# Starting every pair's weight sums early, and in another order, in a two-layer encoder trunk

## The chip, the core and the metric

The kernel runs on one core of one Trainium2 chip. The metric is the device time in microseconds (us) of one execution, the median of several. The engines named below are TensorE (PE, the matmuls), VectorE (DVE), ScalarE (ACT), GpSimd (POOL, here only an issuer of DMAs that add) and SyncE (SP, an issuer of plain loads). Each runs its own instructions strictly in the order of its queue.

## What is computed

528 tokens (16 learned ones and 512 of the input) of 1024 features pass through two layers, each of FFN, mixer, FFN; then a norm. Only the FFNs bear on the change:

```python
def rmsnorm(x, g):
    return x * lax.rsqrt(jnp.mean(x * x, axis=-1, keepdims=True) + EPS) * g

def swiglu(x, w_gate, w_up, w_down):
    return (jax.nn.silu(x @ w_gate) * (x @ w_up)) @ w_down

for l in range(DEPTH):                       # DEPTH = 2
    h = h + 0.5 * swiglu(rmsnorm(h, norm_gains[l, 0]), ffn_w_gate[l, 0], ffn_w_up[l, 0], ffn_w_down[l, 0])
    ...
    h = h + 0.5 * swiglu(rmsnorm(h, norm_gains[l, 2]), ffn_w_gate[l, 1], ffn_w_up[l, 1], ffn_w_down[l, 1])
```

The gate and up matrices are 1024 x 2816, the down matrix 2816 x 1024. The mixer (linear attention beside softmax attention) is the same code before and after.

## The kernel before

**Precision and products.** Operands are split into a high and a low part (`hi`, `lo`), and a product is three matmuls, hi*hi, hi*lo, lo*hi. The weight's high part is a cast on ACT (L343), its low part a subtraction on DVE (L344). The low and high parts live in four rotating buffers each, with one buffer apart for every fifth product, so that the parts of product n can be written when PE has finished product n−5 or so. An FFN is written (l, f): (0, 0), (0, 1), (1, 0), (1, 1).

**Pairs and units.** The 2816 hidden columns are 11 pairs of 256. For a pair, the products of gate and up with the two halves of the tokens are done as a 2 x 2 block product in Winograd's form, with seven products named "1" to "7" in place of eight. Their weights are blocks of the matrix or sums of blocks: "1" is w11, "2" is w12, "4" is w22, "5" is w21 + w22, "6" is s2 = w21 + w22 − w11, "7" is s3 = w21 − w11, and "3" is s4 = s2 − w12. Eight of the pairs also go, two at a time, through such a seven-product form of the down matrix; these are the four units of an FFN, numbered 11 to 14 in the same tables, and their weight sums are made in the same way. A unit is worked in while the pair behind its own two is computed: pairs 2, 4, 6, 8, and 3, 5, 7, 9 in (0, 0), which `lasts` names.

**How a sum is made.** The base, block 21, is loaded by SP into a tile of the pool `ws` (seven buffers), and POOL issues a DMA that adds block 22 onto it (`base`, `base_sum`): that is w21's sum. From w11, ACT writes −w11 into two more tiles (`negative`, L291). POOL's DMAs then add block 21 to one (s3) and w21's sum to the other (s2). In `first_sums` the two negatives come first, and s3's DMA before s2's. s4 starts from w12 likewise and adds s2. A DMA that needs another one's result is held on POOL until that one has landed, and what is behind it in POOL's queue is held too. The product that needs a sum has it cast on ACT like any weight, so the cast is held there until the sum has landed.

**When.** `Weights.use` runs once for each product, in the order of the table `ffn_steps`. It first takes from an agenda what has become due, then makes high and low parts some four products ahead, then fetches two further. The agenda holds (place, what, pair), what being 0 for the base's sum and 1 for `first_sums`. Units and some pairs (those after a last pair, and pair 2 of (0, 0)) are `early` (L251): their base is loaded LEAD = 2 loads sooner, and `first_sums` is issued as soon as w11 is fetched. For all others `first_sums` follows the making of w11's high and low parts (in `make`).

**Around a product.** Each group of matmuls at L749 goes into PSUM; `finished` then copies the partial result with a snapshot on ACT (L759) or adds it on DVE (L764) into one of two buffers of quarters, `c`. A later product that goes on accumulating in the same PSUM tile waits for that snapshot. When a pair's quarters are complete, `hidden` scales them by the norm's factor on DVE (L789), applies Silu on ACT (L512) and multiplies, and splits the result for the down product (L517 for the pairs outside the units). `high_priority` asks the scheduler to put instructions ahead of others in their engine's queue.

**The start.** In (0, 0) pairs 0 and 1 begin without the block form (`first_pair`), and the norm's sums (L541) are a few matmuls issued from inside it, with the factor from Ln, Exp and Square on ACT (L554, L512, L558) behind them. Copies of these pairs' results are at L715.

Of the kernel before, what the change touches and what calls it, by code (L numbers as in the profile page):

```python
# [43 lines left out]
NPAIR = FF // P // 2  # L44
# [21 lines left out]
LEAD = 2  # L66
# [6 lines left out]
def lasts(begin):  # L73
    return [2 * g + begin + 2 for g in range(SEVENS)]


def plains(begin):
    summed = [p for g in range(SEVENS) for p in unit(begin, g)]
    return [p for p in range(NPAIR) if p not in summed]
# [127 lines left out]
class Groups:  # L207


    def __init__(self, tc):  # L210
        self.tc, self.layer, self.groups, self.counts = tc, 0, {}, {}
# [16 lines left out]
class Weights:  # L228
# [3 lines left out]
    def __init__(self, nc, after, raw, hi, lo, wts, win, wdn):  # L232
        self.nc, self.raw, self.hi_pool, self.lo_pool, self.wts, self.win, self.wdn = nc, raw, hi, lo, wts, win, wdn
        self.sum_pool = None
        self.loads = []
        for t, col in zip(PLAN, COLUMN):
            if t[0] == "op":
                self.loads.append(t[1:])
            elif col % SLAB == 0:
                self.loads.append(col // SLAB)  # L240
        self.at = {load: i for i, load in enumerate(self.loads)}
        self.made, self.fetched, self.got, self.summed, self.raws, self.second = 0, 0, {}, {}, {}, {}
        self.pos, self.behind, self.after = 0, None, after
        ops = [i for i, load in enumerate(self.loads) if not isinstance(load, int)]
        self.apart = set(ops[4::5])
        self.extra = self.latest = None
        self.bases, self.agenda = [], []
        for i in ops:
            f, p, product = self.loads[i]
            if product == "1":  # L250
                early = p >= NPAIR or f == (0, 0) and p == 2 or p - 1 in lasts(f == (0, 0))  # L251
                at = i - LEAD * early
                self.bases.append((at, (f, p)))
                self.agenda += [(at, 0, (f, p))] + [(i, 1, (f, p))] * early
        self.bases.sort()
        self.agenda.sort()
# [45 lines left out]
        self.add(self.summed[f, i, "5"], self.dram(f, i, "22"))  # L302

    def first_sums(self, f, i, w):
        s3, s2 = [self.negative(f, i, n, w) for n in ("s3", "s2")]
        self.add(s3, self.dram(f, i, "21"))
        self.add(s2, self.summed[f, i, "5"])
        self.summed[f, i, "7"], self.summed[f, i, "6"], self.second[f, i] = s3, s2, s2

    def last_sum(self, f, i, w):  # L310
# [81 lines left out]
def build(tc, ctx, xt, wts, win, wdn, par, w2, const, umask, out):  # L392
# [13 lines left out]
    def after(ins):  # L406
        return tc.issue_after(ins) if ins is not None else nullcontext()
# [36 lines left out]
    def pair(second=False):  # L444
        return (slots["s2"] if second else pss).tile([P, 2, 512], F32, tag="s2" if second else "ss", name=nm("ss"))
# [65 lines left out]
    def act(*args, **kw):  # L511
        prev_act[0] = S.activation(*args, **kw).ins  # L512

    def split(src, tag_hi, tag_lo):
        n = src.shape[-1]
        hi, lo = slot(tag_hi, F32R, n), slot(tag_lo, F32R, n)
        S.copy(hi, src)  # L517
        V.tensor_tensor(lo, src, hi.bitcast(F32), ALU.subtract)  # L518
        return hi, lo
# [153 lines left out]
    def ffn(l, f, norm, done, following):  # L673

        x, rs, n = norm.x, None, live[0]
        w = n // 2
# [3 lines left out]
        last_pairs, plain_pairs = lasts(begin_block), plains(begin_block)  # L680
# [3 lines left out]
        def put_off(i, fn):  # L684
            later.setdefault(i, []).append(fn)
# [4 lines left out]
        def quarters():  # L690
            return slots["c"].tile([P, 4 * T], F32, tag="c", name=nm("c"))[:, : 4 * n].rearrange("p (j q c) -> p j q c", j=2, q=4)
# [3 lines left out]
        def first_pair(p, m):  # L695

            accs = [pair(m == "1") for _ in range(2)]
            blocks = [W.op((l, f), p, m + c) for c in "12"]
            for r, (hi, lo) in enumerate(blocks):
                for k, (first, second) in enumerate(zip(x, norm.second)):  # L700
                    for j, acc in enumerate(accs):
                        for i, (a, b) in enumerate(((hi, 0), (hi, 1), (lo, 0))):
                            for t, v in enumerate((first, second)):
                                last = TE.matmul(acc[:, t, :w], a[:, j, k], v[b][:, r], start=k == 0 and r == 0 and i == 0,
                                                 stop=k == len(x) - 1 and r == 1 and i == 2)
                    if (p, m, r, k) == (1, "2", 0, 1):
                        with after(last.ins):
                            factor.append(norm.rs("s2", urgent=False))
            st = made.setdefault(p, {})
            if "c" not in st:  # L710
                st["c"] = quarters()
            at = 2 * (m == "2")
            for j, acc in enumerate(accs):
                with tc.high_priority():
                    W.behind = S.copy(st["c"][:, j, at : at + 2], acc[:, :, :w]).ins  # L715
# [37 lines left out]
        def finished(p, product):  # L753
            st = made[p]
            acc = st[{"2": "Y", "5": "Z", "3": "Z"}.get(product, "X")][:, :, :w]

            def snapshot(q):
                with tc.high_priority():
                    snap = S.copy(st["c"][:, :, q], acc).ins  # L759
                if q == 3 and (p == 0 or p in last_pairs):  # L760
                    W.behind = snap

            def more(q, acc):
                V.tensor_tensor(st["c"][:, :, q], st["c"][:, :, q], acc, ALU.add)  # L764

            if product == "1":
                st["c"] = quarters()
                snapshot(0)
            elif product == "2":
                more(0, acc)  # L770
            elif product == "6":
                snapshot(1)
            elif product == "7":
                snapshot(3)
                more(3, st["Z"][:, :, :w])
            elif product == "4":
                hidden(st, p, 1)
            elif product == "3":
                with tc.high_priority() if p in last_pairs else nullcontext():
                    more(1, acc)  # L780
                hidden(st, p, 0)

        def hidden(st, p, m):

            c = st["c"]
            at = slice(2 * m, 2 * m + 2)

            def scale(to, src, cs):
                V.scalar_tensor_tensor(to, src, -0.5, rs[:, cs].unsqueeze(1).broadcast_to([P, 2, cs.stop - cs.start]),  # L789
                                       ALU.mult, ALU.mult)  # L790

            last = p in last_pairs
            at_end = steps.index(("P", p, "3")) if ("P", p, "3") in steps else now[0]
            if m and "X" in st:
                with tc.high_priority() if last else nullcontext():
                    scale(c[:, :, 2], st["X"][:, :, :w], slice(0, w))

            def gate():
                if m and "X" in st:
                    scale(c[:, :, 3], c[:, :, 3], slice(w, n))  # L800
                else:
                    both = c[:, :, at].rearrange("p j q c -> p j (q c)")
                    scale(both, both, slice(0, n))
                t, u = [c[:, j, at].rearrange("p q c -> p (q c)") for j in range(2)]
                act(t, t, AF.Silu)
                V.scalar_tensor_tensor(u, t, 0.5, u, ALU.mult, ALU.mult)
                if p in plain_pairs:
                    hid[2 * p + m] = split(u, *("tt" if p == 0 else "gg"))

            if last:  # L810
                put_off(at_end + (2 if m else 4), gate)
            else:
                gate()
            st["rows"] = st.get("rows", 0) + 1
            if st["rows"] == 2 and p not in plain_pairs:
                for i, piece in enumerate(forms(p, c)):
                    if last or i:
                        put_off((at_end + 6 if last else now[0]) + i, piece)
                    else:
                        piece()  # L820
# [738 lines left out]
```

## Time and profile before

| what | value |
|---|---|
| time, median of 3 runs | 2181.53 us (2181.1 to 2182.91) |
| the profiled execution's own time | 2182.33 us |
| its span in the trace | 2180.6 us |
| mean granted TensorE clock | 0.998 |
| PE busy | 99% of the span |
| DVE busy | 1712.3 us, 79% |
| ACT busy | 1369.9 us, 63% |
| POOL busy | 204.1 us, 9% |
| software DMAs (POOL's queue) | 121.65 MB, 31.3% of the 16 engines' span |
| hardware DMAs (SP's queue) | 195.13 MB, 26.3% |

The span is the time from the first to the last instruction in the trace; what lies outside it is the difference to the execution's time. Busy shares are means over all stages. A wait is idle time of an engine just before an instruction, put down to what ended it. `<-` in a row reads "is written from": `s<-w` on POOL is s2's add, `s<-win` is s3's, and `w<-win` is w21's.

### The profile page before, as it was taken

To read this page: it belongs to the slowest core of one execution; us is meant where nothing else is said; L and a number is where in the kernel's file an instruction comes from. 1 tells how busy PE (TensorE), PEld (TensorE's weight loads), DVE (VectorE), ACT (ScalarE), POOL (GpSimd) and SP (SyncE) were. 2 spreads that over 40 slices of the span, in tenths; PEclk is the share of its full clock that TensorE was granted. 3 is DMA by queue.
4 is the path that set the end of the run, shared out by engine and by line. 5 is a ranking of instruction groups with operands and counts; after the bars stand their busy time and mean duration, and the time that the engine had idled before them with its cause. 6 is when DMAs were issued, how large, how long until landed. Compare 5 with 4: busy or idle time off the path is not lost.

```text
span 2180.6 us, 40542 instructions
## 1 busy us (share of the span) xinstructions
PE 2148.4 (99%) x16572; PEld 2067.0 (95%) x16572; DVE 1712.3 (79%) x2627; ACT 1369.9 (63%) x2022; POOL 204.1 (9%) x236
## 2 busy tenths in 40 slices
PE   9999999999999999999999999999999999999998
PEld 9999999999999999999999999999888888999997
DVE  7888876677976678898689888775789867888885
ACT  8765655455784576666586666554557837666664
POOL 0111100000000011111011111000000001111110
PEclk9999999999999999999999999999999999999999
DMA  7788953211113678888578888632221137888871
GB/s 234 181 202 207 213 136 120 84 59 59 40 40 107 160 167 199 210 199 208 154 171 198 213 199 204 158 126 78 69 68 49 50 115 174 191 207 214 210 182 61
DMA packets 90748, 322.61 MB, mean 148 GB/s; under 512 B 10049, under 2 KB 12353, under 8 KB 90561
## 3 DMA queue, kind: packets, MB, share of 16 engines
q0 software_dynamic: 33408, 121.65, 31.3%
q1 hardware_dynamic: 55072, 195.13, 26.3%
q10 hardware_dynamic: 2080, 3.23, 0.4%
q8 instruction: 130, 2.13, 0.4%
q14 instruction: 58, 0.47, 0.1%
HBM read 257.06 MB, written 2.10 MB: 119 GB/s over the span
## 4 chain that ended last, share of the span: by engine, by line
PE 81%; DVE 6%; ACT 5%; DMA 4%; issue 3%; POOL 0%; SPq 0%; DVEq 0%; ACTq 0%; POOLq 0%
PE ss L749 32%; PE ss L868 14%; PE mm L529 14%; PE ss L529 11%; DMA s<-w 3%; PE sm L529 2%; DVE wlo L344 1%; DMA w<-win 1%; ACT whi L343 1%; PE sm L1238 1%; PE ss L1212 1%; ACT t L512 1%; PE sm L1256 1%; PE sm L1257 1%; PE ss L1213 1%
## 5 line engine op out<-in xcount | busy, mean ns | idle before, releaser
L749 PE MATMUL ss<-xc,whi 128*128 128x264 f32 (+1 forms) x4608 | 842.8, 284 | 11.1 <-ACT c L759 8.9
L749 PEld LDWEIGHTS ss<-xc,whi 128*128 128x128 f32 x4608 | 713.9, 189 | 14.6 <-ACT c L759 11.3
L749 PE MATMUL ss<-xc,wlo 128*128 128x264 f32 (+1 forms) x2304 | 653.8, 284 | 0.0
L749 PEld LDWEIGHTS ss<-xc,wlo 128*128 128x128 f32 x2304 | 434.4, 189 | 0.0
L529 PE MATMUL mm<-x,whi 128*128 128x264 f32 (+1 forms) x1712 | 383.3, 314 | 0.0
L343 ACT CAST whi<-w 128x1024 fp32r<-128x1024 f32 (+1 forms) x241 | 252.1, 1047 | 158.6 <-PE ss L749 64.9
L344 DVE TENSOR_TENSOR wlo<-w,whi 128x1024 fp32r<-128x1024 f32 (+1 forms) x241 | 292.6, 1215 | 56.6 <-ACT whi L343 55.9
L868 PE MATMUL ss<-g,whi 128*128 128x264 f32 (+1 forms) x1792 | 327.0, 283 | 0.0
L344 DVE TENSOR_TENSOR wlo<-s,whi 128x1024 fp32r<-128x1024 f32 x174 | 211.0, 1220 | 126.8 <-ACT whi L343 126.5
L343 ACT CAST whi<-s 128x1024 fp32r<-128x1024 f32 x174 | 180.9, 1047 | 182.5 <-DMA s<-w 102.8
L529 PEld LDWEIGHTS mm<-x,whi 128*128 128x128 f32 x1712 | 278.1, 188 | 15.7 <-DVE x L518 0.2
L868 PEld LDWEIGHTS ss<-g,whi 128*128 128x128 f32 x1792 | 277.0, 188 | 0.0
L529 PE MATMUL mm<-x,wlo 128*128 128x264 f32 (+1 forms) x856 | 264.4, 313 | 0.0
L868 PE MATMUL ss<-g,wlo 128*128 128x264 f32 (+1 forms) x896 | 253.9, 283 | 0.0
L343 ACT CAST whi<-raw 128x1024 fp32r<-128x1024 f32 x126 | 132.0, 1048 | 145.5 <-PE mm L529 69.5
L344 DVE TENSOR_TENSOR wlo<-raw,whi 128x1024 fp32r<-128x1024 f32 x126 | 153.8, 1221 | 78.7 <-ACT whi L343 78.0
L291 ACT ACTIVATE s<-w 128x1024 f32<-128x1024 f32 x174 | 179.9, 1055 | 9.7 <-DMA s<-s 9.7
L868 PEld LDWEIGHTS ss<-g,wlo 128*128 128x128 f32 x896 | 168.7, 188 | 0.0
L529 PEld LDWEIGHTS mm<-x,wlo 128*128 128x128 f32 x856 | 159.6, 188 | 7.4
L872 DVE TENSOR_TENSOR h<-h,ss 128x528 f32<-128x528 f32 (+1 forms) x224 | 153.2, 693 | 2.8
L529 PE MATMUL ss<-g,whi 128*128 128x264 f32 (+1 forms) x764 | 142.8, 302 | 1.3 <-ACT g L517 1.3
L529 PEld LDWEIGHTS ss<-g,whi 128*128 128x128 f32 x764 | 111.6, 188 | 6.9 <-ACT g L517 1.5
(300 smaller groups left out, 3340.6 us busy)
## 6 DMA issues: line engine op xcount, KB each, us to landing
w<-win SPq DMA_DIRECT2D x175, 512.0 KB, 5.7
raw<-wts SPq DMA_DIRECT2D x126, 512.0 KB, 3.4
w<-wdn SPq DMA_DIRECT2D x64, 512.0 KB, 6.8
s<-w POOLq DMA_DIRECT2D x58, 512.0 KB, 7.8
s<-s POOLq DMA_DIRECT2D x58, 512.0 KB, 5.7
w<-win POOLq DMA_DIRECT2D x42, 512.0 KB, 8.1
s<-win POOLq DMA_DIRECT2D x42, 512.0 KB, 7.5
w<-wdn POOLq DMA_DIRECT2D x16, 512.0 KB, 7.2
```

The lines of the kernel that those rows point to most:

```text
L291: self.nc.scalar.activation(t, w, AF.Copy, scale=-1.0)
L343: self.latest = nc.scalar.copy(hi[:, cs], w[:, cs]).ins
L344: nc.vector.tensor_tensor(lo[:, cs], w[:, cs], hi[:, cs].bitcast(F32), ALU.subtract)
L512: prev_act[0] = S.activation(*args, **kw).ins
L529: TE.matmul(acc.half[i][:width], lhs, rhs[:, acc.spans[i]], start=first, stop=last)
L749: TE.matmul(acc[:, j], a[:, j, k], b[:, at], start=bool(begin and k == 0 and i == 0), stop=k == len(x) - 1 and i == 2, skip_group_check=no ...
L868: TE.matmul(acc[:, j], a[:, 2 * half + j, k], b, start=bool(begin and k == 0 and i == 0), stop=k == 1 and i == 2, skip_group_check=not begin)
L872: V.tensor_tensor(to, to, acc, ALU.add)
L1212: TE.matmul(s[:n, i, :HF], lhs, kh[:, hs], start=True, stop=False)
L1213: TE.matmul(s[:n, i, :HF], lhs, kl[:, hs], start=False, stop=True)
L1238: TE.transpose(tp[:, j * w + u * n : j * w + (u + 1) * n], pr[:n, (2 * c2 + j) * P : (2 * c2 + j + 1) * P], ident[:n, :n])
L1256: TE.matmul(o[:, :w], vw, ph, start=i == 0, stop=False)
```

## The change

There are four edits. All pairs but pair 1 become early, so that `first_sums` of pairs 0, 2, 4, 6, 8, 10 (0, 3, 5, 7, 9 in (0, 0)) is issued when w11 is fetched, and the base of those pairs from 2 on is loaded two loads sooner; pair 1's base is loaded one load later. In `first_sums` s2's negative and add now come first, and then s3's. The norm's sums in (0, 0) are issued after the matmuls of k = 2 in place of k = 1, 12 matmuls later. And the last pair, 10, has its last add and its gated values at high priority.

```diff
--- before.py
+++ after.py
@@ -248,8 +248,8 @@
         for i in ops:
             f, p, product = self.loads[i]
             if product == "1":
-                early = p >= NPAIR or f == (0, 0) and p == 2 or p - 1 in lasts(f == (0, 0))
-                at = i - LEAD * early
+                early = p != 1
+                at = i + 1 if p == 1 else i - LEAD * (p > 1)
                 self.bases.append((at, (f, p)))
                 self.agenda += [(at, 0, (f, p))] + [(i, 1, (f, p))] * early
         self.bases.sort()
@@ -302,9 +302,10 @@
         self.add(self.summed[f, i, "5"], self.dram(f, i, "22"))
 
     def first_sums(self, f, i, w):
-        s3, s2 = [self.negative(f, i, n, w) for n in ("s3", "s2")]
+        s2 = self.negative(f, i, "s2", w)
+        self.add(s2, self.summed[f, i, "5"])
+        s3 = self.negative(f, i, "s3", w)
         self.add(s3, self.dram(f, i, "21"))
-        self.add(s2, self.summed[f, i, "5"])
         self.summed[f, i, "7"], self.summed[f, i, "6"], self.second[f, i] = s3, s2, s2
 
     def last_sum(self, f, i, w):
@@ -703,7 +704,7 @@
                             for t, v in enumerate((first, second)):
                                 last = TE.matmul(acc[:, t, :w], a[:, j, k], v[b][:, r], start=k == 0 and r == 0 and i == 0,
                                                  stop=k == len(x) - 1 and r == 1 and i == 2)
-                    if (p, m, r, k) == (1, "2", 0, 1):
+                    if (p, m, r, k) == (1, "2", 0, 2):
                         with after(last.ins):
                             factor.append(norm.rs("s2", urgent=False))
             st = made.setdefault(p, {})
@@ -776,9 +777,10 @@
             elif product == "4":
                 hidden(st, p, 1)
             elif product == "3":
-                with tc.high_priority() if p in last_pairs else nullcontext():
+                with tc.high_priority() if p in last_pairs + [NPAIR - 1] else nullcontext():
                     more(1, acc)
-                hidden(st, p, 0)
+                with tc.high_priority() if p == NPAIR - 1 else nullcontext():
+                    hidden(st, p, 0)
 
         def hidden(st, p, m):
```

Below, before and after are given apart, with the program's numbers in the names. A name such as s2_11_2 is s2 of FFN (1, 1), pair 2.

**ACT in (0, 0), from the cast of pair 2's s2 (product "6") on.** rs53 is the norm's factor, c63 pair 2's quarters, c34 pair 1's. Before:

```order
L343 CAST whi10_645<-s2_00_2_343 128x1024
L554 ACTIVATE rs53_682<-ss56_687,eps_86 128x528
L512 ACTIVATE rs53_682<-rs53_682 128x528
...
L291 ACTIVATE s3_00_3_792<-w11_00_3_651 128x1024
L291 ACTIVATE s2_00_3_794<-w11_00_3_651 128x1024
L759 COPY c63_824<-ss62_787 128x2x264
```

After:

```order
L344 CAST whi10_648<-s2_00_2_341 128x1024
L291 ACTIVATE s2_00_3_654<-w11_00_3_652 128x1024
L291 ACTIVATE s3_00_3_657<-w11_00_3_652 128x1024
L555 ACTIVATE rs53_700<-ss56_705,eps_86 128x528
...
L344 CAST whi12_794<-w11_00_3_652 128x1024
L513 ACTIVATE c34_579<-c34_579 128x528 x2
L518 CAST t60_789<-c21_319 128x528
L344 CAST whi13_839<-s3_00_2_344 128x1024
L344 CAST whi14_875<-w12_00_3_798 128x1024
L760 COPY c63_824<-ss62_793 128x2x264
```

The two negatives of pair 3 (L291) stood behind the norm's steps and the cast of w11; now they stand ahead of them, and the casts whi13 and whi14 and a pair of Silus (c34) stand ahead of the snapshot of c63.

**ACT in (1, 1), pair 2, from a snapshot of the pair before it on.** In (0, 1) and (1, 0) the same rows stand in the same order. Before:

```order
L759 COPY c1748_21433<-ss1734_21334 128x2x256
L343 CAST whi438_21527<-s2_11_1_21258 128x1024
L343 CAST whi440_21605<-w11_11_2_21533 128x1024
L759 COPY c1748_21433<-ss1734_21334 128x2x256
L554 ACTIVATE rs1753_21586<-ss1756_21591,eps_86 128x512
L343 CAST whi439_21601<-w21_11_1_21164 128x1024
L512 ACTIVATE rs1753_21586<-rs1753_21586 128x512
L291 ACTIVATE s3_11_2_21609<-w11_11_2_21533 128x1024
L558 ACTIVATE t1757_21597<-rs1753_21586 128x512
L291 ACTIVATE s2_11_2_21611<-w11_11_2_21533 128x1024
```

After:

```order
L760 COPY c1748_21433<-ss1734_21334 128x2x256
L344 CAST whi438_21530<-s2_11_1_21256 128x1024
L291 ACTIVATE s2_11_2_21560<-w11_11_2_21534 128x1024
L291 ACTIVATE s3_11_2_21563<-w11_11_2_21534 128x1024
L344 CAST whi440_21611<-w11_11_2_21534 128x1024
L760 COPY c1748_21433<-ss1734_21334 128x2x256
L555 ACTIVATE rs1753_21592<-ss1756_21597,eps_86 128x512
L344 CAST whi439_21607<-w21_11_1_21199 128x1024
L513 ACTIVATE rs1753_21592<-rs1753_21592 128x512
L559 ACTIVATE t1757_21603<-rs1753_21592 128x512
```

The two negatives of pair 2 stood among the norm's steps, behind the casts whi440 and whi439, s3's first; now both stand directly behind whi438, s2's first.

**POOL at the same place.** The DMAs that add, of pair 2 of (1, 1). Before:

```order
L296 DMA s4_11_1_21292<-s2_11_1_21258 128x1024
L296 DMA w21_11_2_21531<-win 128x1024
L296 DMA s3_11_2_21609<-win 128x1024
L296 DMA s2_11_2_21611<-w21_11_2_21531 128x1024
L296 DMA s4_11_2_21689<-s2_11_2_21611 128x1024
```

After:

```order
L296 DMA s4_11_1_21292<-s2_11_1_21256 128x1024
L296 DMA w21_11_2_21472<-win 128x1024
L296 DMA s2_11_2_21560<-w21_11_2_21472 128x1024
L296 DMA s3_11_2_21563<-win 128x1024
L296 DMA s4_11_2_21689<-s2_11_2_21560 128x1024
```

s2's add, which waits for w21's to land, now stands ahead of s3's, which does not.

PE has the same instructions as before, and its order changes in few places: in (0, 0) the norm's matmuls stand 12 later, and 17 matmuls of pair 3's product "1" (with whi12) stand ahead of pair 2's "6"; and in each other FFN four matmuls of one product change places with another's, early in pair 2's stretch. POOL has 240 DMAs as before.

## The prediction

> **What bounds the kernel now.** I began with the page's busy times, then asked the chain of waits for TensorE (PE) alone, because an engine that is busy nearly all the time can only give back what it waits.
>
> The page's first row:
>
> ```profile
> PE 2148.4 (99%) x16572; PEld 2067.0 (95%) x16572; DVE 1712.3 (79%) x2627; ACT 1369.9 (63%) x2022; POOL 204.1 (9%) x236
> ```
>
> PE is idle for 2180.6 − 2148.4 = 32.2 us of the span. Nothing but those 32.2 us, and stretches in which PE runs below its full clock, can be won without taking matmuls away, and the change takes none away. The waits of PE, longest first:
>
> ```profile
> PE ss L749 <- ACT c L759: 8.9, 7, 2.8
> PE ss L749 <- DVE c L764: 2.2, 4, 0.7
> PE ss L529 <- ACT g L517: 1.3, 1, 1.3
> PE ss L541 <- ACT c L715: 1.0, 1, 1.0
> ```
>
> Columns: total us, times, longest. These four are in the FFNs, where the change acts: matmuls at L749 wait until ScalarE (ACT) has copied the previous partial sum out of PSUM (the snapshot, L759) or VectorE (DVE) has added to it (L764). The same PE idle time by place, as busy time in the stretches that hold it:
>
> ```profile
> 40.00:50.00 10.00, 8.90 (x71) 8.48 (x71) 8.83 (x16) 9.90 (x17) 1.77 (x2) 1.00 0.98 255
> 70.00:80.00 10.00, 9.41 (x77) 9.20 (x76) 6.42 (x7) 5.67 (x7) 2.66 (x3) 1.00 0.97 229
> 180.00:190.00 10.00, 9.47 (x78) 9.26 (x77) 9.97 (x16) 8.93 (x12) 2.25 (x3) 1.00 1.02 208
> 800.00:812.00 12.00, 9.62 (x62) 9.00 (x61) 11.92 (x17) 8.80 (x12) 2.41 (x3) 0.86 0.95 170
> 1080.00:1090.00 10.00, 8.71 (x72) 8.49 (x71) 7.54 (x9) 7.77 (x10) 2.51 (x3) 1.00 0.68 181
> 1150.00:1160.00 10.00, 8.03 (x64) 7.60 (x63) 9.94 (x15) 7.37 (x11) 1.74 (x2) 1.00 0.97 164
> 1860.00:1880.00 20.00, 15.39 (x126) 14.79 (x125) 14.13 (x19) 12.23 (x17) 3.52 (x4) 1.00 0.85 188
> 2050.00:2060.00 10.00, 8.97 (x76) 8.77 (x76) 7.68 (x9) 8.17 (x10) 2.97 (x4) 1.00 0.83 148
> ```
>
> The first two columns are the stretch's length and PE's busy time; the difference is PE's idle time: 1.10, 0.59, 0.53, 2.38, 1.29, 1.97, 4.61 and 1.03 us, 13.5 in all. The three largest, at 800, 1150 and 1860, are one place of the program in three FFNs, pair 2. ACT's timeline at the largest (start, duration, line; in brackets the idle time before and what ended it):
>
> ```profile
> 1844.10 1.05 ACT L343 CAST whi<-s 128x1024 fp32r<-128x1024 f32 x1
> 1848.40 1.05 ACT L343 CAST whi<-w 128x1024 fp32r<-128x1024 f32 x1 [3.26 <-issue]
> ...
> 1866.77 1.05 ACT L343 CAST whi<-s 128x1024 fp32r<-128x1024 f32 x1 [5.55 <-DMA s<-w]
> ...
> 1871.18 0.58 ACT L759 COPY c<-ss 128x512 f32<-128x512 f32 x1
> ```
>
> The cast of s2 at 1866.77 waits 5.55 us for the sum's DMA, and the snapshot that PE needs stands behind it. The DMA was issued by GpSimd (POOL) only after ACT had made s3's negative and then s2's (start, duration; in brackets again what POOL waited for):
>
> ```profile
> 1842.26 0.89 POOL L296 DMA_DIRECT2D w<-win  x1 [6.24 <-DMA w<-win]
> 1853.34 0.88 POOL L296 DMA_DIRECT2D s<-win  x1 [10.19 <-ACT s L291]
> 1854.81 0.86 POOL L296 DMA_DIRECT2D s<-w  x1 [0.59 <-ACT s L291]
> ```
>
> It took 1866.77 − 1854.81 = 11.9 us. That is long: DMAs from and to the sums' tiles in the 40 us around, and then the load of the DMA engines (last two columns: share, GB/s):
>
> ```profile
> DMA to landing us min/median/max: 4.8/5.5/11.9
> ```
>
> ```profile
> 1848.00:1852.00 4.00, 3.99 (x32) 3.70 (x30) 2.33 (x3) 3.60 (x6) 0.00 (x0) 1.00 0.12 47
> 1852.00:1856.00 4.00, 4.00 (x36) 4.00 (x35) 3.09 (x5) 3.50 (x5) 1.74 (x2) 1.00 0.30 40
> 1856.00:1860.00 4.00, 4.00 (x36) 4.00 (x35) 4.00 (x6) 3.97 (x5) 0.00 (x0) 1.00 0.99 240
> ```
>
> The engines stood nearly empty until 1854, then s3's sum, s2's sum and the next unit's blocks all came at once. A sum issued some 6 us earlier has them to itself. That decides what this change is worth.
>
> **The change part by part.** *Early sums for pair 2, s2 first.* In the new order both negatives stand directly behind the cast at 1844.10, in the 3.26 us that ACT idles there; two of them (1.06 us each by a row below) fit in. POOL then waits only for the landing of the sum issued at 1842.26, 5.5 us in the median and 11.9 at worst, so s2's add goes out at 1848 to 1854. I take 1848, since the DMA share is 0.12 there. It then lands at 1853.5, and at 1860 even with 11.9 us; ACT asks for it at 1866.77 − 5.55 = 1861.2. So the 5.55 us are gone and the snapshot runs as soon as its product is done. Gains, each the whole idle time of its row: 2.38 + 1.97 + 4.61 = 8.96. The row at 2050 is the same thing for pair 8 (its snapshot followed a cast that came late): 1.03. At 70 it is pair 3 of the first FFN: 0.59. At 180 the pair was early already and only s2's place in the queue changes; between 0 and 0.53, I take 0.3.
>
> *What is late next there.* In each of the three places PE had a second wait, for a snapshot into a buffer that the previous pair frees when DVE has made its forms. These become due earlier too, as the gated values stood behind the same stall, but with little to spare. Unknown, between 0 and 1.46 us each; I take 0.4, nearer to zero since what they wait for also moves up: −1.2 in all.
>
> *The clock.* After the stall near 808 PE ran slowly for a while:
>
> ```profile
> 808.44 0.81 PE L749 MATMUL ss<-xc,whi 128*128 128x264 f32 x2 [1.46 <-ACT c L759]
> ...
> 809.26 0.64 PE L749 MATMUL ss<-xc,whi 128*128 128x264 f32 x2
> ...
> 811.89 0.40 PE L749 MATMUL ss<-xc,whi 128*128 128x264 f32 x2
> ...
> 812.25 0.41 PE L749 MATMUL ss<-xc,whi 128*128 128x264 f32 x2
> ```
>
> Three matmuls start every (811.89 − 809.26)/4 = 0.66 us, afterwards every 0.36. The five groups from 808.44 cost 3.45 instead of 1.8 us: 1.6 lost, and the row at 800 shows it as a granted clock of 0.86. No such loss follows the longer stall at 1860 (clock 1.00). I count the 1.6 as gained, since it stands right behind a wait that goes.
>
> The Trainium skill, "TensorE: Matmul & The Clock Gate", section "What's actually happening", states that the clock halves after a whole idle window of about 3.4 us. The trace does not agree: here PE lost the clock after a gap of 1.46 us, and kept it (1.00) in the row that holds its longest, 2.8 us. By the rule alone the slow stretch would not be due to the stall, would stay, and the sum would be 1.6 us less.
>
> *Steady pairs (4, 6, 8 and the like).* Their sums also move up by some 7 us; PE has no wait in those stretches, so nothing is gained. What could be lost is a rival below.
>
> *End of the second FFN.* ACT's timeline, with PE waiting for the gated value at 1085.43:
>
> ```profile
> 1081.56 1.05 ACT L343 CAST whi<-w 128x1024 fp32r<-128x1024 f32 x1 [1.01 <-DMA w<-win]
> ...
> 1084.46 1.06 ACT L291 ACTIVATE s<-w 128x1024 f32<-128x1024 f32 x1
> 1085.43 0.61 ACT L517 CAST g<-c 128x528 fp32r<-128x528 f32 x1
> ```
>
> With the priority, s3's negative goes behind it; s2's takes the place of the cast at 1081.56 and waits for the same block. The value comes 0.97 us sooner: 1.0 of 1.29 us.
>
> *First FFN, norm sums one part on.* PE's wait of 1.0 us at L541 ends when the copy of ACT's first row below has run, at 45.17 + 0.59 = 45.76; the sums now come 12 matmuls later (1.5 us at 0.36 for three), when the copy is done, and the 1.0 is gained. But the early sums of pair 3 now stand ahead of the norm's own activations:
>
> ```profile
> 45.17 0.59 ACT L715 COPY c<-ss 128x528 f32<-128x528 f32 x1
> ...
> 48.17 0.70 ACT L554 ACTIVATE rs<-ss,eps 128x528 f32<-128x528 f32 x1
> ...
> 53.04 0.65 ACT L512 ACTIVATE c<-c 128x528 f32<-128x528 f32 x1 [0.57 <-DVE c L789]
> ...
> 56.99 1.06 ACT L343 CAST whi<-w 128x1024 fp32r<-128x1024 f32 x1
> ...
> 58.96 2.02 ACT L291 ACTIVATE s<-w 128x1024 f32<-128x1024 f32 x2
> 60.88 0.60 ACT L759 COPY c<-ss 128x528 f32<-128x528 f32 x1
> ```
>
> The two at 58.96 occupy ACT until 60.88 (1.9 us). They move to 48.2, so the norm's first step begins at about 50.1; a cast now stands between the norm's steps (1.0), and the scaled values and what follows come some 2.9 us later: the Silu at 53.04 near 55.9, the cast at 56.99 near 59.9, its DVE half near 62. The snapshot of 60.88 also has two more casts (1.9) and two Silus (1.1) ahead of it, and the negatives no longer: 60.88 + 2.9 − 1.9 + 1.9 + 1.1 = 64.9, done at 65.5. PE's next product into that buffer now starts as the snapshot ends, 61.5. Less the 1.0 us that goes it would be there at 60.5; 17 matmuls (2.1 us) of another product, the cast's, now stand ahead of it, so 62.6. PE waits 65.5 − 62.6 = 2.9 us, for the cast's halves first and the snapshot then: net −1.9. From both sides: nothing if DVE and ACT catch up, 4 us if the cast's lateness, some 1.5 for PE, comes on top instead of running beside the snapshot's.
>
> The sum: 8.96 + 1.03 + 0.59 + 0.3 + 1.0 + 1.6 − 1.2 − 1.9 = 10.4 us. From the profiled execution's 2182.33 us (span 2180.6 and 1.7 outside it) that is 2171.9; the median of the runs, 2181.53, lies 0.8 lower, so I predict 2171.1.
>
> **The rivals.** *A new stall early on, and clock lost elsewhere.* The first FFN pays 4 us (net −3), the second waits stay whole (3 x 1.46 = 4.4), and the 1.6 of clock is lost at a new place: 11.9 − 3 − 4.4 = 4.5 gained, 2181.5 − 4.5 = 2177.0. For it: ACT is busy for 9.90 of 10 us at 40. Against: in the next stretch shown, at 70, it is busy for 5.67.
>
> *The sum is still late.* If POOL is held at the head of its queue until the pair's first sum lands, and that landing takes 11.9 us too, s2's add leaves at 1854.2, when it left before, and lands at 1866: PE's waits of pair 2 and the slow clock stay, and of the rest come 1.03 + 0.59 + 1.0 − 1.9 = 0.7 us: 2180.8. Against: the empty DMA engines at 1848. The Trainium skill, "DMA: Bandwidth & Descriptors", section "Issuing engines are not separate DMA queues", says that all queues interleave on the same 16 engines; the row at 1856 (0.99) agrees.
>
> *Slower: negatives ahead of what they wait for.* 23 more pairs (five in the first FFN, six in each other) have negatives on ACT that wait for a freshly loaded block, with casts and snapshots behind them. The page's row of these loads, then the load of a steady pair's block (SyncE) and the ACT row behind which its negatives now stand:
>
> ```profile
> w<-win SPq DMA_DIRECT2D x175, 512.0 KB, 5.7
> ```
>
> ```profile
> 832.52 0.33 SPq L285 DMA_DIRECT2D w<-win  x1
> ```
>
> ```profile
> 842.17 1.05 ACT L343 CAST whi<-s 128x1024 fp32r<-128x1024 f32 x1 [1.20 <-DMA s<-w]
> ```
>
> The load lands after 5.7 us in the median; the negatives come 843.2 − 832.5 = 10.7 us after its issue. Up to there nothing happens. If loads grew to 11.9 us, the longest seen here, each of the 23 would hold ACT for 1.2 us, and as PE is 99% busy up to 28 us would come back: 2171.1 + 28 = 2199. It outweighs the gain of 10.4 us from 10.7 + 10.4/23 = 11.2 us on. Against: 5 us of reserve.
>
> *The change does nothing*, the stalls only passing to the next wait: it is the second rival's time, and counted there.
>
> **How the numbers follow.** Forecast 0.62, early stall and lost clock 0.17, sum still late 0.14, slower 0.07. About 0.2% (4.4 us) is what a measurement of this kernel can tell from no change. The first two are faster by more than that, except for the weakest part of the early stall: faster 0.78, same 0.15, slower 0.07. The lower end takes all 13.5 us, the clock's 1.6, and a new stall of nothing: 15.1, 2166.4, rounded to 2166.0. The upper end takes in the early stall's 2177.0 with 1.5 us more for a longer one, 2178.5; beyond it lie most of the two last rivals.
>
> **What would show it.** Right: no ACT wait on "DMA s<-w" before the cast of s2 in pair 2 of the last three FFNs; PE's waits on L759 down from 8.9 to about 3, most of it near 61 to 65; a granted clock of 1.00 at 808; POOL's s2 sum issued near 1848 in its stretch; PE's wait at L541 gone. Wrong: ACT waiting on "DMA w<-win" in steady pairs, PE's total busy time grown by slow clock, or the waits near 800, 1150 and 1860 still there under another name.

## The result and the profile after

The changed kernel takes 2168.1 us (median of 6 runs, 2166.94 to 2168.73) against 2181.32 for the kernel before (6 runs): a ratio of 0.9938, 95% interval 0.9925 to 0.9951. That is 13.2 us less; 10.4 were forecast. Between the two profiled executions it is 2182.33 − 2168.02 = 14.3 us.

The page's first row of the changed kernel, and PE's waits in the FFNs. Line numbers are one or two higher than before (L749 is now L750, L759 is L760):

```profile
PE 2145.2 (99%) x16572; PEld 2066.7 (95%) x16572; DVE 1714.5 (79%) x2627; ACT 1370.5 (63%) x2022; POOL 204.7 (9%) x236
```

```profile
PE ss L750 <- DVE c L765: 1.5, 3, 0.9
...
PE ss L750 <- DVE wlo L345: 0.8, 1, 0.8
...
PE ss L530 <- ACT g L518: 0.4, 1, 0.4
```

The span is 2166.2 us, so PE idles 21.0 us in place of 32.2. The 8.9 us of waits for a snapshot are gone altogether, the 2.2 for DVE's add and the 1.0 at L541 too, and 1.3 became 0.4. New are 0.8 us for a weight's low part, near 60 us, and 1.5 us for DVE's add in three places, all in the last FFN.

ACT in pair 2 of the last FFN, the place whose rows of before stand in the prediction:

```profile
1834.21 1.05 ACT L344 CAST whi<-s 128x1024 fp32r<-128x1024 f32 x1
1835.16 2.00 ACT L291 ACTIVATE s<-w 128x1024 f32<-128x1024 f32 x2
...
1838.47 1.05 ACT L344 CAST whi<-w 128x1024 fp32r<-128x1024 f32 x1 [1.30 <-PE ss L750]
...
1852.22 2.19 ACT L344 CAST whi<-s 128x1024 fp32r<-128x1024 f32 x2
...
1857.14 0.58 ACT L760 COPY c<-ss 128x512 f32<-128x512 f32 x1
```

The negatives fill the gap of 3.26 us, as the order had them, and the cast at 1852.22 no longer waits. POOL there, and how long the two adds took to land (the last column):

```profile
1838.45 0.87 POOL L296 DMA_DIRECT2D s<-w  x1 [5.27 <-DVE t L537]
1839.01 1.21 POOL L296 DMA_DIRECT2D s<-win  x1
```

```profile
s<-w POOLq DMA_DIRECT2D x1, 512.0 KB, 4.8
s<-win POOLq DMA_DIRECT2D x1, 512.0 KB, 9.3
```

s2's add lands 4.8 us after its issue in place of 11.9, 9 us before ACT wants it. Up to here the forecast reads well. The experiments show that moving the sums up was one of two ways to this, and not needed.

### The profile page after: what moved, and what is told of

Same layout as the page of the kernel before. It is cut to its first block, busy times and chain, and to the rows that moved or that the text cites. A ratio compares the mean times of both kernels' runs of the same rounds, so it can differ in the third digit from the quotient of the medians.

```text
span 2166.2 us, 40569 instructions
## 1 busy us (share of the span) xinstructions
PE 2145.2 (99%) x16572; PEld 2066.7 (95%) x16572; DVE 1714.5 (79%) x2627; ACT 1370.5 (63%) x2022; POOL 204.7 (9%) x236
## 4 chain that ended last, share of the span: by engine, by line
PE 83%; DVE 7%; ACT 4%; DMA 3%; issue 2%; SPq 0%; POOL 0%; DVEq 0%; POOLq 0%; ACTq 0%
PE ss L750 35%; PE mm L530 14%; PE ss L870 13%; PE ss L530 11%; PE sm L530 3%; DMA w<-win 1%; DMA s<-w 1%; DVE wlo L345 1%; PE sm L1240 1%; DMA w<-wdn 1%; PE ss L732 1%; ACT t L513 1%; PE ss L1214 1%; PE sm L1258 1%; ACT whi L344 1%
## 5 line engine op out<-in xcount | busy, mean ns | idle before, releaser
L750 PE MATMUL ss<-xc,whi 128*128 128x264 f32 (+1 forms) x4608 | 839.9, 284 | 1.5 <-DVE c L765 1.5
L750 PEld LDWEIGHTS ss<-xc,whi 128*128 128x128 f32 x4608 | 712.6, 188 | 3.2 <-DVE c L765 2.2
L750 PE MATMUL ss<-xc,wlo 128*128 128x264 f32 (+1 forms) x2304 | 653.2, 284 | 0.8 <-DVE wlo L345 0.8
L750 PEld LDWEIGHTS ss<-xc,wlo 128*128 128x128 f32 x2304 | 433.6, 188 | 1.0 <-DVE wlo L345 1.0
L870 PEld LDWEIGHTS ss<-g,whi 128*128 128x128 f32 x1792 | 277.1, 188 | 0.0
L291 ACT ACTIVATE s<-w 128x1024 f32<-128x1024 f32 x174 | 178.1, 1053 | 1.2 <-DMA w<-win 1.1
L296 POOL DMA_DIRECT2D w<-win x42 | 44.2, 1053 | 812.9 <-DVE g L519 383.1
```

The costliest lines, as they stand in the source:

```text
L291: self.nc.scalar.activation(t, w, AF.Copy, scale=-1.0)
L296: self.nc.gpsimd.dma_start(t, src, accum_op=ALU.add)
L750: TE.matmul(acc[:, j], a[:, j, k], b[:, at], start=bool(begin and k == 0 and i == 0), stop=k == len(x) - 1 and i == 2, skip_group_check=no ...
L870: TE.matmul(acc[:, j], a[:, 2 * half + j, k], b, start=bool(begin and k == 0 and i == 0), stop=k == 1 and i == 2, skip_group_check=not begin)
```

## The experiments

### Each edit alone

The first edit alone, on the kernel before:

```diff
-                early = p >= NPAIR or f == (0, 0) and p == 2 or p - 1 in lasts(f == (0, 0))
-                at = i - LEAD * early
+                early = p != 1
+                at = i + 1 if p == 1 else i - LEAD * (p > 1)
```

> The kernel before with the first edit alone: all pairs but pair 1 early, s3 still ahead of s2 in the queue, norm sums and priorities as before. Early theory (the sum leaves sooner because its negative stands in ACT's gap): PE's waits on the snapshot at about 800, 1150 and 1860 us are gone (9 us), the slow clock at 808 too (1.6), the stretch near 60 us gets a wait of 1 to 3 us and the 1.0 at 45 stays; the time is 9 to 12 us below the kernel before. Queue theory (s2's place ahead of s3 does it): half of those waits or more stay, 5 us or less below.

Measured: 2171.23 us, ratio 0.9957 (0.9944 to 0.9969), 9.9 us less than the 2181.16 beside it. The waits of pair 2 are gone; the first FFN has three waits, at 46, 62 and 64 us (1.4, 0.6, 1.4 us).

The second edit alone:

```diff
-        s3, s2 = [self.negative(f, i, n, w) for n in ("s3", "s2")]
+        s2 = self.negative(f, i, "s2", w)
+        self.add(s2, self.summed[f, i, "5"])
+        s3 = self.negative(f, i, "s3", w)
         self.add(s3, self.dram(f, i, "21"))
-        self.add(s2, self.summed[f, i, "5"])
```

> The kernel before with the second edit alone: s2's negative and add ahead of s3's, nothing earlier otherwise. Early theory: s2's add leaves 1.5 us sooner and still meets the same crowd of transfers, so ACT's wait for it in pair 2 of the last FFN falls from 5.55 to some 3 to 4 us and PE keeps most of its waits there; 2 to 5 us below the kernel before. Queue theory: the waits at 800, 1150 and 1860 go, 9 us or more below.

Measured: 2166.62 us, ratio 0.9939 (0.9926 to 0.9951), 14.5 us less. So this edit alone does what the whole change does, and the expectation of 2 to 5 us was wrong. The waits of pair 2 are gone although no sum is started at an earlier product. The two gains are the same gain: either edit removes the wait, and together they can't remove it twice.

The other two edits alone:

```diff
-                    if (p, m, r, k) == (1, "2", 0, 1):
+                    if (p, m, r, k) == (1, "2", 0, 2):
```

> The kernel before with the third edit alone, the norm sums 12 matmuls later. Both theories: the 1.0 us wait at 45 us goes, or half of it comes back a little later; all else stays: 0 to 1 us below the kernel before, which the measurement can't tell. Its waits of pair 2 stay, and show whether the slow clock follows them again: if it follows any stall, it shows at one or more of 808, 1157, 1872 us; if it is tied to the first, at 808 alone.

```diff
-                with tc.high_priority() if p in last_pairs else nullcontext():
+                with tc.high_priority() if p in last_pairs + [NPAIR - 1] else nullcontext():
                     more(1, acc)
-                hidden(st, p, 0)
+                with tc.high_priority() if p == NPAIR - 1 else nullcontext():
+                    hidden(st, p, 0)
```

> The kernel before with the fourth edit alone, the last pair's gated values at high priority. The wait of 1.3 us for the gated value at 1086 falls to 0.3 to 0.5; all else stays, 1 us below the kernel before, within what can be measured. Its waits of pair 2 stay, and are a second look at the slow clock.

Measured: norm sums later 2181.25 us, ratio 1.0008 (0.9999 to 1.0017); priority 2181.21 us, ratio 1.0002 (0.9993 to 1.0011). Neither moves the time by itself. With the norm sums later, the wait at 45 us goes, and 2.6 + 0.6 us of waits come a little later in the first FFN. The priority leaves the wait for the gated value at 1.2 us; it was expected to fall to 0.3 to 0.5.

### Undoing parts of the change

Pair 2 of the last three FFNs late again:

```diff
-                early = p != 1
-                at = i + 1 if p == 1 else i - LEAD * (p > 1)
+                early = p != 1 and not (p == 2 and f != (0, 0))
+                at = i + 1 if p == 1 else i - LEAD * (p > 1 and early)
```

> The changed kernel with pair 2 of the last three FFNs not early (its base two loads later as before, its sums behind the making of w11), all else changed. Early theory: ACT waits for s2's DMA in these three places again and PE for the snapshot, 5 to 9 us and perhaps the slow clock come back: 2173 to 2179. Queue theory: s2 is still first in the queue, so the time stays within 2 us of 2168.

Measured: 2169.82 us (0.9952, 0.9939 to 0.9964), 1.7 us above the changed kernel, though the intervals of the two ratios overlap; of its waits on the snapshot 0.2 us is back. So at the very place on which the forecast rested, moving the sums up isn't needed once s2 goes first.

No first edit at all, the other three kept:

```diff
-                early = p != 1
-                at = i + 1 if p == 1 else i - LEAD * (p > 1)
+                early = p >= NPAIR or f == (0, 0) and p == 2 or p - 1 in lasts(f == (0, 0))
+                at = i - LEAD * early
```

> The changed kernel without its first edit: only the units and the pairs that were early before are early; s2 first, norm sums later and the priority stay. If the queue place does the work and the early sums add nothing that PE waits for, the three waits of pair 2 stay gone, the waits at 1908 and 1968 and the one near 60 us are gone too, and the time is 2164 to 2167. If the early sums bring a part of their own, it is 2169 or more.

Measured: 2166.6 us (0.9936, 0.9923 to 0.9948; 2165.28 to 2166.97 in 5 runs), 1.5 us below the changed kernel, with no wait at all between 30 and 100 us and none on DVE's add. The kernel before took 2180.54 us beside it, 0.8 less than beside the changed kernel, so the two ratios can't be told apart. In the traces the span is 2165.1 us against 2166.2, with one stretch of slow clock near 550 us in each: there the early sums cost a little more than they bring.

### What s2 first changes on the chip

In the kernel before, s3's and s2's adds and two plain loads (SyncE, the next unit's blocks) are issued within 1.5 us. Their landing times, first of the kernel before, then of s2 first alone:

```profile
w<-wdn SPq DMA_DIRECT2D x2, 512.0 KB, 8.3
s<-win POOLq DMA_DIRECT2D x1, 512.0 KB, 5.4
s<-w POOLq DMA_DIRECT2D x1, 512.0 KB, 11.9
```

```profile
w<-wdn SPq DMA_DIRECT2D x2, 512.0 KB, 8.5
s<-w POOLq DMA_DIRECT2D x1, 512.0 KB, 5.5
s<-win POOLq DMA_DIRECT2D x1, 512.0 KB, 10.6
```

The two adds change places; the loads land about as before (8.5 us in place of 8.3). Over the whole program the page's medians say the same, before and with s2 first alone:

```profile
s<-w POOLq DMA_DIRECT2D x58, 512.0 KB, 7.8
...
s<-win POOLq DMA_DIRECT2D x42, 512.0 KB, 7.5
```

```profile
s<-w POOLq DMA_DIRECT2D x58, 512.0 KB, 5.5
...
s<-win POOLq DMA_DIRECT2D x42, 512.0 KB, 10.3
```

s3 pays, and has the time: PE has no wait for it in this kernel. I took this for the place in POOL's queue alone, and tested that by exchanging the two adds on POOL and leaving ACT's order as it was:

```diff
         s3, s2 = [self.negative(f, i, n, w) for n in ("s3", "s2")]
-        self.add(s3, self.dram(f, i, "21"))
-        self.add(s2, self.summed[f, i, "5"])
+        first = self.nc.gpsimd.dma_start(s2, self.summed[f, i, "5"], accum_op=ALU.add).ins
+        with self.after(first):
+            self.add(s3, self.dram(f, i, "21"))
```

> The kernel before with the two adds of first_sums exchanged on GpSimd alone; on ScalarE s3's negative still comes first, so s2's add can leave no sooner than before. Whole-transfer theory (a sum second in GpSimd's queue lands only after the first one's transfer, 5.4 against 11.9 us in the kernel before): s2's add lands 5 to 6 us after its issue, the waits on the snapshot at 800, 1150 and 1860 go, and the time is 11 to 14 us below the kernel before, like that of s2 first. Rival (what counts is that the negative and so the issue come 1.5 us sooner): s2 still lands late and the gain is 4 us or less.

Measured: 2175.56 us, ratio 0.998 (0.9971 to 0.9989), 5.0 us less: the whole-transfer theory falls as it was put. In pair 2 of the last FFN:

```profile
w<-wdn SPq DMA_DIRECT2D x2, 512.0 KB, 5.1
s<-w POOLq DMA_DIRECT2D x1, 512.0 KB, 9.3
```

```profile
1859.02 1.05 ACT L344 CAST whi<-s 128x1024 fp32r<-128x1024 f32 x1 [2.93 <-DMA s<-w]
```

First in its queue s2 still needs 9.3 us, and now the loads are quick. Halving what stands ahead of it in the kernel before:

```diff
-        self.add(s3, self.dram(f, i, "21"))
+        self.add(s3[:64], self.dram(f, i, "21")[:64])
```

> The kernel before, with s3's add moving 64 of the 128 partitions: it leaves out half of that sum, so that what stands ahead of s2's add in the queue is half as large, and the order of everything stays. Theory (s2's transfer waits for the bytes ahead of it): s2's add lands about 2.5 us sooner than in the kernel before where the two leave together (11.9 to about 9.5 us in pair 2 of the last FFN, ACT's wait there 5.55 to about 3), and a third to two thirds of the 13 us come back: 2172 to 2177. Rival (what counts is the order or the number of transfers, not their size): s2 still lands at 11 us or later there, and the time stays at 2180 or above.

Measured: 2176.22 us, ratio 0.9975 (0.9964 to 0.9985), 5.1 us less. s2 lands after 10.2 us and ACT waits 3.85 in place of 5.55: the bytes ahead count, but by less than expected. The next run leaves s3's add out:

```diff
-        self.add(s3, self.dram(f, i, "21"))
```

> The kernel before without s3's add: it leaves that sum out, so s2's add has nothing ahead of it or beside it in GpSimd's queue, and leaves at the same place of ACT's order as before, 0.4 us behind two plain loads of the next unit (SyncE's queue). If s3 alone makes s2 late, s2 lands after 5.5 us in pair 2 of the last FFN and all waits there go, 12 to 14 us below the kernel before. If the two loads ahead of it cost it as well, as in the kernel with the queue exchanged (9.3 us, loads 5.1), s2 still lands after 8 us or more there, some of PE's waits stay, and the time is 5 to 9 us below the kernel before.

Measured: 2172.15 us, ratio 0.9961 (0.9947 to 0.9975), 8.3 us less. POOL, SyncE and ACT in pair 2 of the last FFN:

```profile
1847.94 0.87 POOL L296 DMA_DIRECT2D s<-w  x1 [13.19 <-ACT s L291]
```

```profile
1847.56 0.80 SPq L285 DMA_DIRECT2D w<-wdn  x2
```

```profile
1857.32 1.05 ACT L342 CAST whi<-s 128x1024 fp32r<-128x1024 f32 x1 [2.96 <-DMA s<-w]
```

With nothing else in POOL's queue s2 still takes 9.3 us, since two loads left 0.4 us ahead of it. So, at this place: 5.5 us when s2 leads, 9.3 with the loads ahead, 11.9 with the loads and s3 ahead. The first edit alone fits in: there s3's add leaves at 1839.13, s2's at 1841.80, the loads at 1843.32, and s2 lands after 5.9 us. And why the loads leave just then shows in ACT, SyncE and POOL of s2 first alone:

```profile
1843.55 1.05 ACT L291 ACTIVATE s<-w 128x1024 f32<-128x1024 f32 x1
...
1845.02 1.06 ACT L291 ACTIVATE s<-w 128x1024 f32<-128x1024 f32 x1
```

```profile
1846.10 1.26 SPq L285 DMA_DIRECT2D w<-wdn  x2
```

```profile
1845.01 0.87 POOL L296 DMA_DIRECT2D s<-w  x1 [10.85 <-ACT s L291]
1846.47 0.87 POOL L296 DMA_DIRECT2D s<-win  x1 [0.60 <-ACT s L291]
```

The second negative ends at 1846.08 and the loads are issued at 1846.10: it is the last reader of w11, and frees the buffer that they wait for. SyncE's waits name it, in the kernel before as well:

```profile
SPq L285 <- ACT s L291: 3.7, 1, 3.7
```

In the kernel before the last negative is s2's, so the same event lets go the loads and, 0.4 us later, s2's add (SyncE in the kernel before; s2's add was at 1854.81):

```profile
1854.43 0.85 SPq L285 DMA_DIRECT2D w<-wdn  x2
```

With s2's negative first, its add leaves 1.1 us ahead of the loads. That is the edit's worth here. The Trainium skill, "DMA: Bandwidth & Descriptors", section "Queues, rings and completion order", states that each engine goes round between the queues packet by packet. By an even share, an estimate from that rule, an add 0.4 us behind two loads would not end long after them; in the run without s3 it landed 9.3 us after its issue, the loads 4.3 and 6.0 after theirs. At this place whoever comes first was served first, beyond an even share; why is not shown.

### What the early sums cost and bring

Pairs 4, 6 and 8 of the last FFN late again:

```diff
-                early = p != 1
-                at = i + 1 if p == 1 else i - LEAD * (p > 1)
+                early = p != 1 and not (f == (1, 1) and p in (4, 6, 8))
+                at = i + 1 if p == 1 else i - LEAD * (p > 1 and early)
```

> The changed kernel with pairs 4, 6 and 8 of the last FFN not early. The changed kernel's trace shows PE waiting 0.92 and 0.36 us for a DVE add (L765) in the last FFN at 1908 and 1968, and it loses 2.2 us there against the kernel before. Theory: the two negatives, now ahead of the cast of the previous unit's form on ACT (1.9 us), make DVE's forms and the add behind them late; then these waits go, the wait of 1.0 us on the snapshot at about 2040 returns for pair 8, and the time is 2166 to 2167. Rival: the waits come from pair 2's faster stretch ahead of them, and stay; the time is 2168 to 2169.5.

Measured: 2166.81 us (0.9937, 0.9923 to 0.995), and PE has no FFN wait left between 1800 and 2100 us; the 1.5 us are gone, and the wait for pair 8's snapshot didn't return. The time lies 1.3 us below the changed kernel, but the runs of the two overlap. The chain in the changed kernel, pair 4, ACT, then DVE, then PE:

```profile
1897.02 2.00 ACT L291 ACTIVATE s<-w 128x1024 f32<-128x1024 f32 x2
1898.93 0.60 ACT L831 CAST g<-c 128x512 fp32r<-128x512 f32 x1
```

```profile
1907.60 0.69 DVE L765 TENSOR_TENSOR c<-c,ss 128x512 f32<-128x512 f32 x1
```

```profile
1907.15 0.28 PE L750 MATMUL ss<-xc,wlo 128*128 128x256 f32 x1
1908.34 0.51 PE L750 MATMUL ss<-xc,whi 128*128 128x256 f32 x2 [0.92 <-DVE c L765]
1908.68 0.28 PE L750 MATMUL ss<-xc,wlo 128*128 128x256 f32 x1
...
1909.04 0.28 PE L750 MATMUL ss<-xc,wlo 128*128 128x256 f32 x1
```

The early negatives stand ahead of the cast of the previous pair's form (L831), DVE's forms and the add behind them come later, and PE waits for the add. With these pairs late, PE does the same matmuls 2.8 us later by the trace's time, yet the cast and the add are no later:

```profile
1897.91 0.62 ACT L831 CAST g<-c 128x512 fp32r<-128x512 f32 x1
```

```profile
1907.74 0.68 DVE L765 TENSOR_TENSOR c<-c,ss 128x512 f32<-128x512 f32 x1
```

Against PE they come 3.8 and 2.7 us sooner, and there is no wait, which shows the cause.

The last kernel keeps the first edit for pair 0 of the last three FFNs only:

```diff
-                early = p != 1
-                at = i + 1 if p == 1 else i - LEAD * (p > 1)
+                early = p >= NPAIR or f == (0, 0) and p == 2 or p - 1 in lasts(f == (0, 0))
+                at = i - LEAD * early
+                early = early or p == 0 and f != (0, 0)
```

> The changed kernel with its first edit for pair 0 of the last three FFNs alone; every other pair is early only where it was before. Theory: the wait for the gated value at the end of the second FFN (1.3 us before, 0.4 in the changed kernel, 1.4 without the first edit and 1.2 with the priority alone) is shortened by the early sums of the next FFN's pair 0, not by the priority; then it is about 0.5 here, the waits of the first FFN, of pair 2 and of the last FFN's steady pairs stay gone, and the time is 1 us below the kernel without the first edit: 2165 to 2166.5. Rival (the other early pairs are needed for it): the wait stays at 1.4 and the time at 2166.6.

Measured: 2165.4 us (2164.57 to 2165.8), ratio 0.9925 (0.9912 to 0.9939), the lowest median of all kernels. The wait for the gated value, with the priority alone, without the first edit, and here:

```profile
PE ss L529 <- ACT g L517: 1.2, 1, 1.2
```

```profile
PE ss L530 <- ACT g L518: 1.4, 1, 1.4
```

```profile
PE ss L531 <- ACT g L519: 0.4, 1, 0.4
```

The early sums of the next FFN's pair 0 shorten it. Before, the cast of its w11 (1081.56 in the prediction's rows) and one negative stood ahead of the gated value's cast on ACT; now one negative stands in that cast's place, and the other behind the gated value. The priority, alone or with s2 first, doesn't.

## Why the forecast held, step by step

The direction and the range held; the middle was 3.0 us high, two reasons behind the right sizes were wrong, and a part of the closeness is luck, as errors cancelled.

- *Pair 2, 8.96 us:* came in full. The mechanism, a sum that leaves ahead of the crowd, is right. The 6 us by which it was to leave earlier were not needed: 1.5 us on POOL, which puts it ahead of two loads, do it as well. The prediction read the crowd after 1854 correctly, but took the order of the two adds for worth a fraction of a us ("only s2's place in the queue changes", 0.3 of 0.53) where it is worth all of it. The right question to the trace was which event lets the loads go.
- *What is late next, −1.2:* nothing was; the second waits went with the first.
- *The clock, 1.6:* came at 808, with some luck. The slow stretches follow the stalls: kernels that keep the stalls show slow stretches at one, two or all of the three places. Three rows of the kernel with the priority alone (the third number from the right is the granted clock):

```profile
808.00:812.00 4.00, 4.00 (x23) 4.00 (x22) 2.98 (x5) 0.98 (x2) 0.00 (x0) 0.57 1.05 214
1156.00:1160.00 4.00, 4.00 (x21) 4.00 (x22) 3.44 (x5) 1.43 (x2) 0.00 (x0) 0.57 1.03 207
1874.00:1878.00 4.00, 3.43 (x19) 3.23 (x18) 3.92 (x7) 4.00 (x7) 1.74 (x2) 0.67 0.60 87
```

Six kernels keep full or partial waits at the three places (before, norm sums later, priority, queue exchanged, half of s3's add, none of it). Of these 18 cases 10 were followed by a slow stretch, and no kernel without the waits had one there. So it was right to count a gain, and the rule of the Trainium skill ("TensorE: Matmul & The Clock Gate", section "What's actually happening"), by which 1.6 us less would have come, doesn't hold here: waits under 3 us were enough. But a wait brings the loss only about every second time.

The profiled execution of the changed kernel has a slow stretch too, at a new place, the mixer of the first layer:

```profile
548.00:552.00 4.00, 4.00 (x28) 3.90 (x28) 2.26 (x5) 2.54 (x6) 0.00 (x0) 0.74 0.00 0
552.00:556.00 4.00, 4.00 (x31) 3.95 (x29) 3.68 (x12) 2.01 (x6) 0.00 (x0) 0.83 0.00 0
```

No wait of PE stands within 10 us ahead of it. The kernel without the first edit has one at the same place (0.59 from 548 to 552), the other eleven traces have none, and what sets it off is open. It costs 0.9 us: the matmul that waits 0.4 us for ACT at 535.37 starts 2.34 us sooner than in the kernel before (537.71), the one at 571.94 only 1.45 us sooner (573.39). So between these two executions, both with a mean clock of 0.998, most of the 1.6 is lost again. Over the runs the clock did rise: its mean is 0.998 or 0.999 in all six runs of the changed kernel, and 0.996 to 0.998 in the 27 of the kernel before that stand beside one set of experiments.

- *Pairs 8 and 3, and the one at 180 us, 1.03 + 0.59 + 0.3:* all three waits are gone, the last with its full 0.53.
- *The gated value, 1.0:* 0.9 came, but from pair 0's early sums and not from the priority.
- *The first FFN, −1.9:* the 1.0 at 45 us went; the new wait is 0.8 us in place of 2.9, so the balance is about +0.2. That is luck of this trace. The norm's first step on ACT began at 48.07 us and not at the 50.1 of the prediction, because ACT had waited 1.86 us for a load near 25 us, 3.32 in the kernel before, and ran 2 us ahead from there on. In two kernels with the same first FFN as the changed one ACT waited 3.62 and 3.29 us for that load, and PE 1.4 + 0.8 and 1.4 + 0.7 us near 60 us, with a slow stretch behind: not far from the forecast. PE's waits and the clock of the kernel with pair 2 late:

```profile
PE ss L750 <- DVE wlo L345: 1.4, 1, 1.4
PE ss L750 <- ACT whi L344: 0.8, 1, 0.8
```

```profile
62.00:66.00 4.00, 3.17 (x18) 3.17 (x19) 4.00 (x6) 4.00 (x6) 0.00 (x0) 0.75 0.54 152
```

- *Steady pairs, nothing:* this step failed. They cost 1.5 us of waits in the last FFN, not by a late load, as the rival had it, but through the cast on ACT and DVE's add behind it. The prediction named the casts behind the moved negatives, but counted a cost only where a load comes late; the 2.0 us that two negatives occupy ACT themselves it put at nothing.

With the sizes put right the sum is 10.4 + 1.2 + 2.1 + 0.2 − 0.1 − 1.5 = 12.3 us, and with the 0.9 lost at 550 us it is 11.4 of the 14.3 us between the profiled executions. Where the rest lies shows when the matmuls of both traces are counted from the start. The lead is by how much sooner the same matmul starts in the changed kernel:

| place | idle time of PE that went (us) | growth of the lead (us) |
|---|---|---|
| first FFN, to 100 us | 0.88 | 1.35 |
| 180 to 210 | 0.53 | 0.99 |
| 550, slow stretch of the changed kernel | 0 | −0.89 |
| 808, with the slow stretch of the kernel before | 2.38 | 4.73 |
| 1086 | 0.87 | 0.87 |
| 1157 | 1.97 | 2.56 |
| 1720 | 0 | 0.27 |
| 1870 | 4.61 | 5.46 |
| pairs 4, 6 and 8 of the last FFN | −1.5 | −2.34 |
| 2060 | 1.03 | 1.30 |

Apart from the clock (1.6 gained, 0.89 lost) the lead grows by 2.8 us more than idle time went. A wait costs more than its idle time: the matmuls otherwise overlap, and the first ones behind it are slow (0.51 us for a pair that otherwise takes 0.40). The rows at 1908 above show that: from 1907.15 to 1908.68 it is 1.53 us, and the next such step, to 1909.04, takes 0.36, so the wait cost 1.17 us where 0.92 are shown as idle. At 0.25 us each, the eight FFN waits fewer (13 before, 5 after) would make 2.0 us, which is an estimate; the other 0.8 us stay open. The prediction, which took idle time and slow clock for all that could be won, put this at nothing.

The rivals: the early stall came at 0.8 us in place of the 4 of the first rival, its lost clock at a new place came in this one execution and cost 0.9, and its second waits didn't come. The sum was not late. A load held a moved negative up at one place, 1.1 us at 1075, where a cast had waited 1.0 us for it before.

## What to carry to other kernels

Before moving work earlier, ask which event lets go the transfers that crowd the late one. Here the last reader of a buffer freed two loads and the urgent sum at once; reading the buffer for the urgent sum first gave the whole gain, and moving 23 pairs' sums up on top of it brought nothing more (in the traces it cost 1.1 us). When two edits remove the same wait, price each alone: the sum of their gains is not there. And before a gain is explained from two traces, look in both for stretches of slow clock that have nothing to do with the change.

## What the runs showed of the hardware

A 512 KB add from POOL landed after 5.5 us when it led, 9.3 with two loads of 512 KB issued 0.4 us ahead in another queue, and 11.9 with another add ahead as well. The clock granted to TensorE fell to half for some 3.4 us (0.57 over a stretch of 4 us) after waits of under 3 us in 10 of 18 cases, never at these places in a kernel without the waits; in two of 13 traces it also fell in the first mixer, near 550 us, with no wait within 10 us ahead. A wait of 0.92 us delayed the matmuls behind it by 1.17 us. The runs of the kernel before spread over some 6 us (2177.67 to 2183.53 in 27 runs beside one set of experiments), those of the changed kernel and of s2 first alone over less than 2. The clock goes with it: of the 27, the ten with a mean clock of 0.996 took 2181.6 us on average, the ten with 0.997 took 2180.3, the seven with 0.998 took 2179.2. Slow stretches that come and go would do that; that they are all of the spread is not shown.
